# The last projection of a hybrid encoder layer: operand sums moved from DRAM to on-chip memory, weight blocks loaded fewer times, residual added by DMA

## The chip, the cores and the metric

The kernel runs on one core of a Trainium2 chip. The metric is the device time of one execution in microseconds (us); the median of several runs is quoted. A profile is one further execution, taken by the hardware profiler.

## What is computed

The reference is one layer of a bidirectional encoder with 512 tokens and a width of 2048, in float32: an input projection, a Mamba-2 style branch, an attention branch, a gated merge, one output product with a residual, and a last RMSNorm. The part that the change touches is its end:

```python
merged = jax.nn.sigmoid(g_ssm) * (y @ w_proj_ssm) + jax.nn.sigmoid(g_attn) * (o @ w_proj_attn)
return x + merged @ w_out
...
return rmsnorm(x, final_norm_w)
```

`merged` is 512 x 2048 and `w_out` is 2048 x 2048.

## The kernel before

**Engines and splitting.** TensorE (PE) multiplies, VectorE (DVE) and ScalarE (ACT) do elementwise work, GpSimd (POOL) a little of it, and SP issues plain loads. Float32 operands are split into a high and a low part, each of a type that PE takes in one pass, and a product is three matmuls (high x high, high x low, low x high). The high part of a weight chunk is a cast on ACT (`wh`, L434) and the low part a subtraction on DVE (`wl`, L435). So each chunk of 128 x 1024 weights costs one ACT and one DVE instruction before PE can use it.

**Strassen.** Each of the three 2048-wide projections at the end (`wps`, `wpa`, `wo`) is done by the class `Strassen` (L612) with seven block products in place of eight, in Winograd's form. Tokens are halved, the inner dimension is halved, and the output columns are taken in two pairs, `cp` 0 and 1, each of which is halved again. A block product (`product`, L571) is four weight chunks of 512 KB by two banks of 128 tokens: 48 matmuls of 128 x 512. The operands made of the input are x11, x12, x21, x22 and the sums S1 to S4. The weight blocks are W11, W12, W21 and W22, and the sums are T1 = W11 + W12, T2 = T1 + W22, T3 = W22 + W12 and T4 = T2 + W21. (Signs are folded in elsewhere.) P1 takes x11 and W11; P2 x12 and W21; P5 S1 and T1; P6 S2 and T2; P3 S4 and W22; P7 S3 and T3; P4 x22 and T4.

**Weight tiles.** On-chip tiles for weights come in rings: four `X` (T1, T2 and T4 are made in place in them), four `Y` (W22, then T3), and three `wraw`, a ring that raw operands also use. T1 and T3 are made by a second DMA that adds into the tile (`w_more`, L511, issued by POOL, L514). T2 (L716) and T4 (L720) are additions on DVE. For `wps` and `wpa`, T1 and T3 are prepared early in DRAM scratch.

**The order in the output product before.** `wo` first runs a head (L673): P1 and P2 for cp 0, then P1 and P2 for cp 1 (named P1b and P2b), which need only x11 and x12. Then `pair` runs P5, P6, P3, P7, P4 for cp 0 and the same five for cp 1. For this W11 of cp 0 is loaded twice (for P1 and again for T1), W21 twice for each cp, and T1 of cp 1 is written to DRAM scratch (`T_wo`, jobs in `t_jobs`, L486, issued by POOL when P5 of cp 0 is done) and read back.

**The operands before.** `done_pa` (L1439) ends each block of `wpa`: gate, add, and, one product later, eight transposes on PE (`turn`, L1446) whose result gives pieces of x11, x12, x21 or x22 of the merged matrix. Pieces of x11, x12 and x22 are split at once or reloaded; the sums S1 to S4 are put together in DRAM (`m_d`) by DMAs that add (L1455, L1462), with two copies of S3 inside DRAM as starting values of S2 and S4 (L1475), and each sum is then read back into raw tiles and split. The last piece, of x22, is turned when P1 of `wo` is through, so S1, S2 and S4 are complete only after that. The tiles for turned pieces, for gates and for residual blocks are one ring of three (`st`, L382).

**The residual before.** For each of the 16 output blocks of 128 x 512, `fetch_o` (L1588) loads the block of x into an `st` tile, DVE adds it (L1607), ACT squares it for the norm (L1600), and POOL multiplies it by the last gain (L1603). Of the two blocks of the last product (`last_o`, L1633) the addition is done before the product. `finish` (L1618) normalises 128 tokens and stores them.

**What orders the work.** PE runs in program order. On the other engines a scheduler orders by program order and by given priorities (`AHEAD`, `LOAD_AHEAD`), and `keep_in_program_order` holds an instruction at its place. Each engine's queue, SP's and POOL's DMA issues among them, is then carried out strictly in order. `hooks` name work to be put behind a given product, as in

```python
wo = Strassen("wo", m_ops, -1, done_o, fetch_o, {
    (0, "P1"): [s_loads], (0, "P2"): [lambda: wo.first_columns(0, nc.sync, True)],
    (1, "P1"): [MC("S1"), MC("S2"), LP(m_ops, "S4")], (0, "P5"): [MC("S4"), final_weights, t_made],
    (1, "P3"): [lambda: finish(0)], (1, "P7"): [lambda: finish(1)]}, kept_o, last_o)
run(wo.head())
run(wo.pair(0, True))
run(wo.pair(1, True))
```

Of the kernel before, what the change touches and what calls it, by code (L numbers as in the profile page):

```python
# [72 lines left out]
def build(tc, a):  # L73
# [48 lines left out]
    m_d = {w: scratch(f"m_{w}", 2048) for w in ("x11", "S1", "S2", "S3", "S4")}  # L122
# [4 lines left out]
    t_d["wo", 1, "T1"] = scratch("T1_wo1", 4096)  # L127
# [323 lines left out]
    class Ops:  # L451


        def __init__(self, src, blocked=False):
            self.src, self.raws, self.view, self.blocked = src, {}, {}, blocked
# [4 lines left out]
        def split(self, which, op, in_order=False):  # L460
            for q, t in enumerate(self.raws.pop(which)):
                ks = slice(4 * q, 4 * q + 4)
                h, l, raw = op[:, 0, ks], op[:, 1, ks], view4(t)
                i = split_into(h, l, raw, -1 if which == "S2" else 1)
                if in_order:
                    tc.keep_in_program_order(i)
            self.see(which, op)

        def see(self, which, op):
            if self.blocked:  # L470
                op = op.rearrange("p s (q t k) (u c) -> p s q t (k u) c", q=2, t=2, u=2)
                self.view[which] = lambda s, j, i: op[:, s, j // 4, i, j % 4]
            else:
                self.view[which] = lambda s, j, i: op[:, s, j, i * P:(i + 1) * P]
# [137 lines left out]
    class Strassen:  # L612
# [35 lines left out]
        def first_columns(self, cp, queue=nc.sync, both=False):  # L648

            self.ahead[cp] = [self.columns(w_tile("X"), cp, m, queue, both) for m in range(4)]  # L650

        def columns(self, t, cp, m, queue=nc.sync, both=False):

            if self.made(cp, "T1"):
                return t_load(t, self.w, cp, "T1", m, queue)
            w_load(t, self.w, cp, 0, 0, m)
            if both:
                w_more(t, self.w, cp, 0, 1, m, LOAD_AHEAD)
            return t
# [13 lines left out]
        def head(self):  # L673

            a = evict((yield from self.first(0, "P1")), "p1")
            self.hook(0, "P1")
            yield from self.second(0, a, lambda i: self.kept("C11", 0)("p5", i))
            self.hook(0, "P2")
            b = evict((yield from self.first(1, "P1b")), "kk")
            self.hook(1, "P1")  # L680
            self.p1 = (a, b)
            yield from self.second(1, b, lambda i: self.kept("C11", 1)("p5", i), None, "P2b")
            self.hook(1, "P2")

        def pair(self, cp, headed=False):
# [8 lines left out]
            if headed:  # L694
                p1 = self.p1[cp]
            else:
                p1 = evict((yield from product(
                    "P1", self.op("x11"), (lambda m: w_load(w_tile("X"), w, cp, 0, 0, m)) if made else column,
                    None if made else lambda m, raw: w_more(raw, w, cp, 0, 1, m))), "p1")
                self.hook(cp, "P1")  # L700

# [25 lines left out]
            def t3(m, raw):  # L727
                w_more(raw, w, cp, 0, 1, m)
                if headed:
                    t4_alone(m, raw)  # L730
# [4 lines left out]
            u = p1 if headed else [sum_tile("u") for _ in range(2)]  # L735
# [4 lines left out]
            if not headed:  # L740
# [698 lines left out]
    def done_pa(t, b, o):  # L1439
# [3 lines left out]
        def turn():  # L1443
# [3 lines left out]
            o_ = st("turned")  # L1447
            w, q = f"x{t // 2 + 1}{b // 2 + 1}", 2 * (b % 2) + t % 2
            d = {n: m_d[n][:, q * SEQ:(q + 1) * SEQ] for n in m_d}
            if b < 2:  # L1450
                act.copy(o_, tp)
                for n in ("x11", "S3") if t < 2 else ("S1",):
                    put(d[n], o_)
                if t >= 2:
                    pool.dma_start(d["S3"], o_, accum_op=ALU.add)  # L1455
            else:
                h, l = (m_op[w][:, s_, 2 * q:2 * q + 2].rearrange("p k t -> p (k t)") for s_ in range(2))
                act.activation(o_, tp, AF.Copy, scale=-1.0)
                act.activation(h, tp, AF.Copy, scale=-1.0)
                dve.scalar_tensor_tensor(l, tp, -1.0, h.bitcast(F32), ALU.mult, ALU.subtract)  # L1460
                for n in ("S4",) if t < 2 else ("S1", "S2", "S4"):
                    pool.dma_start(d[n], o_, accum_op=ALU.add)  # L1462
# [3 lines left out]
    m_op = {}  # L1466
    m_ops = Ops(m_d, True)

    def m_place(w):
        def f():  # L1470
            m_op[w] = slot(w)
            m_ops.see(w, m_op[w])
        return f

    def m_copies():  # L1475
        for n in ("S2", "S4"):
            tc.keep_in_program_order(pool.dma_start(m_d[n], m_d["S3"]))

    def MC(w):
        return lambda: m_ops.split(w, m_op[w], True)  # L1480
# [3 lines left out]
    def o_sums(n, i=1):  # L1484
# [12 lines left out]
        (1, "P1"): [LP(m_ops, "x11"), m_place("x11")], (1, "P5"): [MC("x11"), m_place("S1")],  # L1497
        (1, "P6"): [m_place("S2"), m_copies], (1, "P2"): [m_place("x12"), LP(m_ops, "S3")],
        (1, "P3"): [m_place("S3")], (1, "P7"): [m_place("x22"), MC("S3"), m_place("S4")]})
# [86 lines left out]
    res, room = {}, {}  # L1586

    def fetch_o(t, b):  # L1588
        fetched[t, b] = st("gate")
        pool.dma_start(fetched[t, b], a["x"][t * P:(t + 1) * P, b * SEQ:(b + 1) * SEQ])  # L1590

    def kept_o(tag, cp, i):
        if tag == "C11":
            return sum_tile(("p5", "ms")[cp])
        if "big" not in room:
            room["big"] = xa.tile([P, 2, 2, 2, SEQ], F32, tag="opa", bufs=2, name="big")
        return room["big"][:, int(tag == "C22"), cp, i]

    def squares(t, b):
        act.activation(fetched.pop((t, b)), res[t, b], AF.Square, accum_out=ssf[:, t, b:b + 1])  # L1600

    def weigh(t, b):
        pool.tensor_mul(res[t, b], res[t, b], room["fw"][:, b])  # L1603

    def done_o(t, b, o):
        res[t, b] = o
        dve.tensor_add(o, o, fetched[t, b])  # L1607
        squares(t, b)
        if "fw" in room:
            weigh(t, b)  # L1610

    def final_weights():
        room["fw"] = xa.tile([P, 4, SEQ], F32, tag="opa", bufs=2, name="fw")
        act.dma_start(room["fw"], a["fnw"].rearrange("o (b n) -> o b n", b=4).broadcast_to([P, 4, SEQ]))
        for t, b in list(res):
            weigh(t, b)

    def finish(t):  # L1618
# [4 lines left out]
        for b in (2, 0, 1, 3):  # L1623
            o = res[t, b]
            if b == 2 and t >= 2:
# [23 lines left out]
    def s_loads():  # L1649
        with tc.high_priority(offset=AHEAD):  # L1650
            for w in ("S1", "S2"):
                m_ops.raws[w] = [col_tile("Y", "xraw") for q in range(2)]
                for q in range(2):
                    pool.dma_start(m_ops.raws[w][q], m_d[w][:, q * 1024:(q + 1) * 1024])

    wo_jobs = t_jobs("wo")

    def t_made():
        while wo_jobs:
            tc.keep_in_program_order(wo_jobs.popleft()())  # L1660

    wo = Strassen("wo", m_ops, -1, done_o, fetch_o, {
        (0, "P1"): [s_loads], (0, "P2"): [lambda: wo.first_columns(0, nc.sync, True)],
        (1, "P1"): [MC("S1"), MC("S2"), LP(m_ops, "S4")], (0, "P5"): [MC("S4"), final_weights, t_made],
        (1, "P3"): [lambda: finish(0)], (1, "P7"): [lambda: finish(1)]}, kept_o, last_o)
    run(wo.head())
    run(wo.pair(0, True))
    run(wo.pair(1, True))
# [69 lines left out]
```

## Time and profile before

| | us |
|---|---|
| median of 3 runs | 2063.26 |
| lowest, highest | 2059.05, 2070.34 |
| the profiled execution, its own time | 2067.23 |
| span of that execution's profile (first to last instruction) | 2065.5 |
| busy: PE, DVE, ACT, POOL | 1952.0, 1539.9, 1004.5, 377.8 |

Every time in a profile counts from the start of its span. A line of a view of waits names who waited, at which line of the kernel, for whom, with the total, the count and the longest wait in us. A line of the chain gives start, duration and what the time went to. "Issue" in the chain is time in which the engine waited for nothing that the profile shows. The granted clock (PEclk) is the share of PE's full clock. The DMA share is the mean busy share of 16 DMA engines.

### The profile page before, as it was taken

Reading aid. Unit: us, or ns where it says so; the run is one execution under the profiler, and the core shown is the slowest. Engines: PE = TensorE matmul, PEld = TensorE weight load, DVE = VectorE, ACT = ScalarE, POOL = GpSimd, SP = SyncE. Lnnn points to the kernel's source line nnn. Section 1 sums busy time; section 2 is a strip of 40 time slices with the busy share of each in tenths; the row PEclk is TensorE's granted clock in tenths of the full one; section 3 lists DMA queues with packets and bytes.
Section 4 is the critical chain, followed back from the end, with each engine's and each line's share of the span. In section 5 each row is a group of like instructions: output and inputs, shape, how many; then the busy total and the mean of one; then the engine's idle time right before and its main releaser. Section 6 shows DMA issues by size and latency. Waiting matters only on the chain.

```text
span 2065.5 us, 24821 instructions
## 1 busy us (share of the span) xinstructions
PE 1952.0 (95%) x8978; PEld 1605.2 (78%) x8978; DVE 1539.9 (75%) x2018; ACT 1004.5 (49%) x1398; POOL 377.8 (18%) x417
## 2 busy tenths in 40 slices
PE   6999999999999999999999999999999999987877
PEld 4878888888878788787788888888777778875666
DVE  7976676676669799898794866767577888774767
ACT  6444444444445646546455444444445445443344
POOL 0001010010032252332520111100120110131222
PEclk9999999999999999999999999999999999998989
DMA  5467657657547757687465966953587886889575
GB/s 195 166 177 200 177 122 190 192 120 177 143 165 196 216 164 210 204 248 227 143 188 173 250 166 178 246 134 93 148 275 221 277 326 232 283 245 278 153 204 138
DMA packets 172074, 404.79 MB, mean 196 GB/s; under 512 B 17104, under 2 KB 62288, under 8 KB 171728
## 3 DMA queue, kind: packets, MB, share of 16 engines
q1 hardware_dynamic: 104976, 239.38, 35.3%
q0 software_dynamic: 36032, 121.13, 26.4%
q10 hardware_dynamic: 30944, 42.71, 5.7%
q8 instruction: 70, 1.15, 0.2%
q14 instruction: 52, 0.43, 0.1%
HBM read 344.95 MB, written 110.62 MB: 221 GB/s over the span
## 4 chain that ended last, share of the span: by engine, by line
PE 64%; DVE 15%; DMA 10%; issue 6%; ACT 4%; POOL 1%; ACTq 0%; SPq 0%; DVEq 0%; POOLq 0%
PE P L588 10%; PE P L589 10%; PE P L587 10%; DVE wl L435 3%; PE za L169 2%; PE za L170 2%; PE za L171 2%; DVE sum L1078 2%; PE xbc L169 2%; PE xbc L170 2%; PE xbc L171 2%; DVE wl L165 1%; DMA m_S<-turned 1%; PE pb L1355 1%; DMA wraw<-wo 1%
## 5 line engine op out<-in xcount | busy, mean ns | idle before, releaser
L434 ACT CAST wh<-X 128x1024 fp32r<-128x1024 f32 x172 | 180.6, 1053 | 201.0 <-PE P L589 151.8
L435 DVE TENSOR_TENSOR wl<-X,wh 128x1024 fp32r<-128x1024 f32 x172 | 212.5, 1239 | 85.8 <-ACT wh L434 85.1
L165 DVE TENSOR_TENSOR wl<-wraw,wh 128x1024 fp32r<-128x1024 f32 (+2 forms) x148 | 177.2, 1198 | 83.5 <-ACT wh L164 81.3
L164 ACT CAST wh<-wraw 128x1024 fp32r<-128x1024 f32 (+2 forms) x150 | 145.0, 969 | 129.9 <-PE xbc L170 35.4
L435 DVE TENSOR_TENSOR wl<-Y,wh 128x1024 fp32r<-128x1024 f32 x96 | 118.3, 1234 | 85.6 <-ACT wh L434 85.6
L434 ACT CAST wh<-Y 128x1024 fp32r<-128x1024 f32 x96 | 101.0, 1053 | 147.5 <-PE P L589 102.7
L169 PE MATMUL xbc<-h_h,wh 128*128 128x512 f32 x384 | 151.6, 395 | 0.0
L171 PE MATMUL xbc<-h_h,wl 128*128 128x512 f32 x384 | 149.9, 390 | 0.0
L170 PE MATMUL xbc<-h_l,wh 128*128 128x512 f32 x384 | 149.7, 390 | 0.0
L587 PE MATMUL P<-wh,h_h 128*128 128x512 f32 x384 | 149.4, 389 | 0.0
L588 PE MATMUL P<-wl,h_h 128*128 128x512 f32 x384 | 149.4, 389 | 0.0
L589 PE MATMUL P<-wh,h_l 128*128 128x512 f32 x384 | 149.4, 389 | 0.0
L435 DVE TENSOR_TENSOR wl<-wraw,wh 128x1024 fp32r<-128x1024 f32 x64 | 78.2, 1223 | 59.4 <-ACT wh L434 59.4
L434 ACT CAST wh<-wraw 128x1024 fp32r<-128x1024 f32 x64 | 67.3, 1052 | 108.2 <-PE P L589 53.0
L588 PE MATMUL P<-wl,S 128*128 128x512 f32 x288 | 112.4, 390 | 0.8 <-DVE wl L435 0.6
L589 PE MATMUL P<-wh,S 128*128 128x512 f32 x288 | 112.1, 389 | 0.0
L587 PE MATMUL P<-wh,S 128*128 128x512 f32 x288 | 112.0, 389 | 0.0
L169 PE MATMUL za<-h_h,wh 128*128 128x512 f32 x256 | 101.5, 396 | 0.0
L170 PE MATMUL za<-h_l,wh 128*128 128x512 f32 x256 | 99.9, 390 | 0.0
L171 PE MATMUL za<-h_h,wl 128*128 128x512 f32 x256 | 99.9, 390 | 0.0
L1078 DVE TENSOR_TENSOR_SCAN sum<-da,scn 128x512 f32<-128x512 f32 x64 | 86.3, 1362 | 0.0
L1342 ACT ACTIVATE pr<-s,nm 128x512 f32<-128x512 f32 x64 | 44.1, 689 | 84.6 <-DVE nm L1340 83.8
(726 smaller groups left out, 5292.0 us busy)
## 6 DMA issues: line engine op xcount, KB each, us to landing
wraw<-wi SPq DMA_DIRECT2D x102, 512.0 KB, 4.0
T_wps<-wps POOLq DMA_DIRECT2D x32, 512.0 KB, 6.2
da<-da_d SPq DMA_DIRECT2D x64, 256.0 KB, 4.5
T_wpa<-wpa POOLq DMA_DIRECT2D x32, 512.0 KB, 9.4
wraw<-wps SPq DMA_DIRECT2D x24, 512.0 KB, 5.9
wraw<-wo SPq DMA_DIRECT2D x24, 512.0 KB, 6.1
xbc_d<-xbc ACTq DMA_DIRECT2D x24, 256.0 KB, 3.1
wraw<-wun SPq DMA_DIRECT2D x16, 384.0 KB, 3.2
```

The lines of the kernel that those rows point to most:

```text
L164: act.copy(h, raw)
L165: (dve if ahead[0] else pool).tensor_sub(l, raw, h.bitcast(F32))
L169: pe.matmul(out, wh, xh, start=start, stop=False)
L170: pe.matmul(out, wh, xl, start=False, stop=False)
L171: pe.matmul(out, wl, xh, start=False, stop=stop)
L434: i = act.copy(hi_, raw)
L435: dve.tensor_sub(lo_, raw, hi_.bitcast(F32))
L587: pe.matmul(bs[i], xh, wh, start=(j == 0), stop=False)
L588: pe.matmul(bs[i], xh, wl, start=False, stop=False)
L589: pe.matmul(bs[i], xl, wh, start=False, stop=(j == 7))
L1078: dve.tensor_tensor_scan(sums[dd], flat(da), mask, 0.0, ALU.add, ALU.mult)
L1342: act.activation(pr, s, AF.Exp, bias=nm, scale=SCALE, accum_out=sm_)
```

## The change

- **Order.** The head is gone. For cp 0 the order is P1, P2, P5, P6, P3, P7, P4, and for cp 1 it is P1, P5, P6, P2, P3, P7, P4. PE does the same 14 products.
- **Weights.** P1 loads W11 straight into the X tiles; W12 is added into them by DMA for T1 while P1 runs. In cp 1, W21 is loaded once, for P2 and T4 together; in cp 0 it is still loaded twice. No T1 goes through DRAM.
- **Operands.** Only x11, x21 and S3 still go to DRAM. Raw tiles of S1 (from x21), S2 and S4 (from S3) and S3 are loaded from there; S4's in one place of the operand ring that also holds the raw of x22. The turned pieces of x12 are added by DMA into S4's raw tile on chip; the pieces of x22 are subtracted from S1's raw tile by DVE straight out of PE's banks, written to x22's raw tile, and added by DMA into the raw tiles of S2 and S4. S2 is split behind P2 of cp 0, S4 and x22 behind P5, S3 behind P6.
- **Residual.** For 12 of the 16 blocks POOL issues a DMA that adds x into the finished block, and ACT squares it one product later. Only the four blocks of the last 256 tokens and columns of cp 1 keep the old way. The last gain is loaded behind P2 of cp 1 instead of P5 of cp 0; for the first 256 tokens it is multiplied in by DVE in `finish`.

The core of the diff:

```diff
-    m_d = {w: scratch(f"m_{w}", 2048) for w in ("x11", "S1", "S2", "S3", "S4")}
+    m_d = {w: scratch(f"m_{w}", 2048) for w in ("x11", "x21", "S3")}
...
-    t_d["wo", 1, "T1"] = scratch("T1_wo1", 4096)
...
+        def load(self, which, src, tiles):
+            self.raws[which] = tiles
+            for q, t in enumerate(tiles):
+                tc.keep_in_program_order(pool.dma_start(t, src[:, q * 1024:(q + 1) * 1024]))
+
+        def raw(self, which, q, t):
+            return self.raws[which][q][:, t * SEQ:(t + 1) * SEQ]
+
+        def into(self, which, raw, c0, n):
+            h, l = (self.tile[which][:, s_, c0:c0 + n] for s_ in range(2))
+            return split_into(h, l, raw, -1 if which == "S2" else 1)
+
+        def split(self, which):
+            for q, t in enumerate(self.raws.pop(which)):
+                tc.keep_in_program_order(self.into(which, t, q * 1024, 1024))
...
-        def pair(self, cp, headed=False):
+        def pair(self, cp, headed=False, early=False):
...
                     None if made else lambda m, raw: w_more(raw, w, cp, 0, 1, m))), "p1", self.kept("p1", cp))
                 self.hook(cp, "P1")
+                if early:
+                    yield from self.second(cp, p1, lambda i: self.kept("C11", cp)("p5", i))
+                    self.hook(cp, "P2")
...
                 w_more(raw, w, cp, 0, 1, m)
-                if headed:
+                if early:
                     t4_alone(m, raw)
...
+            elif t < 2:
+                o_ = st("turned")
+                act.activation(o_, tp, AF.Copy, scale=-1.0)
+                pool.dma_start(m_ops.raw("S4", q, u), o_, accum_op=ALU.add)
+                m_ops.into(w, o_, sl.start, SEQ)
             else:
...
+                s1, raw = (m_ops.raw(n, q, u) for n in ("S1", "x22"))
+                dve.tensor_sub(s1, s1, tp)
+                act.activation(raw, tp, AF.Copy, scale=-1.0)
+                m_ops.into("S1", s1, sl.start, SEQ)
+                for n in ("S2", "S4"):
+                    pool.dma_start(m_ops.raw(n, q, u), raw, accum_op=ALU.add)
...
+        (1, "P1"): [m_place("x11"), m_load("x11", "x11", w_raw)], (1, "P5"): [m_split("x11"), m_room],
+        (1, "P6"): [m_place("S1")], (1, "P2"): [m_place("x12")], (1, "P3"): [m_place("S2")],
+        (1, "P7"): [m_place("S4"), m_load("S1", "x21", y_tile), m_load("S2", "S3", y_tile)],
+        (1, "P4"): [m_place("x22")]})
...
     def done_o(t, b, o):
         res[t, b] = o
-        dve.tensor_add(o, o, fetched[t, b])
-        squares(t, b)
-        if "fw" in room:
+        if late(t, b):
+            dve.tensor_add(o, o, fetched[t, b])
+            squares(t, b)
             weigh(t, b)
+            return
+        pool.dma_start(o, x_of(t, b), accum_op=ALU.add)
+
+        def then():
+            squares(t, b)
+            if "fw" in room:
+                weigh(t, b)
+            if b == 3:
+                finish(t)
+
+        after(1, then)
...
     wo = Strassen("wo", m_ops, -1, done_o, fetch_o, {
...
+        (0, "P2"): [m_split("S2")],
+        (0, "P5"): [m_split("S4", "x22"), m_place("S3"), m_load("S3", "S3", w_raw)],
+        (0, "P6"): [m_split("S3")], (1, "P2"): [final_weights]}, kept_o, last_o)
+    run(wo.pair(0, early=True))
+    run(wo.pair(1))
```

More of the change, by code (lines that the diff above doesn't have):

```diff
@@ new lines, in done_pa, with m_place, m_room, m_load @@
+        after(1, turn)
+    m_ops = Merged()
+    def m_place(*which):
+        return lambda: [m_ops.place(w, slot(w)) for w in which]
+    def m_room():
+        t = xb.tile([P, 4, 1024], F32, tag="opb", bufs=4, name="m_raw")
+        n_places[0] += 1
+        m_ops.raws["x22"] = [t[:, q] for q in range(2)]
+        m_ops.load("S4", m_d["S3"], [t[:, 2 + q] for q in range(2)])
+    def m_load(w, src, tile_):
+        return lambda: m_ops.load(w, m_d[src], [tile_("xraw") for q in range(2)])
+    def y_tile(name):
+        return col_tile("Y", name)
```

131 lines of the change are left out of this document (50 added, 81 removed).

## The prediction

> **What bounds the kernel now.** I read the page first, then the busy time by stretch, the waits of PE, the chain, and the waits of the other engines.
>
> ```profile
> span 2065.5 us, 24821 instructions
> ## 1 busy us (share of the span) xinstructions
> PE 1952.0 (95%) x8978; PEld 1605.2 (78%) x8978; DVE 1539.9 (75%) x2018; ACT 1004.5 (49%) x1398; POOL 377.8 (18%) x417
> ```
>
> PE is busy for 95% of the span, so only stretches where it starves can give time back. I looked for them by cutting the output product at its block products. In order the rows are P1, P2, P1b, P2b, P5 with P6, P3, P7 (all cp 0), and the last row holds six products: P4 of cp 0 and all five of cp 1.
>
> ```profile
> core 0: us, PE busy (x) PEld busy (x) DVE busy (x) ACT busy (x) POOL busy (x), PEclk, DMA share, GB/s
> 1841.20:1861.90 20.70, 14.42 (x58) 11.19 (x57) 8.70 (x11) 7.01 (x9) 8.31 (x11) 0.84 1.05 311
> 1861.90:1873.20 11.30, 11.30 (x52) 9.07 (x51) 6.19 (x6) 6.25 (x10) 5.89 (x7) 1.00 1.09 278
> 1873.20:1897.80 24.60, 13.32 (x49) 9.86 (x47) 6.18 (x8) 5.57 (x9) 4.24 (x8) 0.83 0.90 285
> 1897.80:1923.70 25.90, 18.23 (x48) 12.62 (x49) 13.78 (x12) 9.76 (x11) 0.00 (x0) 0.77 0.55 171
> 1923.70:1945.50 21.80, 21.80 (x97) 18.02 (x96) 18.84 (x17) 12.53 (x16) 8.30 (x6) 1.00 0.34 120
> 1945.50:1959.10 13.60, 11.40 (x49) 8.74 (x47) 11.07 (x11) 3.15 (x3) 6.26 (x9) 1.00 0.94 254
> 1959.10:1986.90 27.80, 14.54 (x49) 10.92 (x50) 10.18 (x11) 6.69 (x9) 7.08 (x8) 0.75 0.99 251
> 1986.90:2052.80 65.90, 65.66 (x289) 53.77 (x287) 57.62 (x73) 34.63 (x50) 19.49 (x19) 1.00 0.51 141
> ```
>
> The last row is the yardstick: six products in 65.90 us with PE busy throughout, 10.98 us each. The whole output product takes 2052.80 - 1841.20 = 211.6 us. Fourteen products at 10.98 are 153.8. Behind P1 come the last eight transposes,
>
> ```profile
> 1861.15 1.04 PE L1446 MATMUL turn<-cst,u 128*128 128x128 f32 x8
> ```
>
> whose end overlaps with the next matmul, so I allow 0.8 for them, which makes 154.6. So **57.0 us are lost**: about 9 in P1 (20.7 less 11.0 and 0.8), 13.6 in P1b, 14.9 in P2b, 2.6 in P3 and 16.8 in P7. The clock column belongs to this: it falls to 0.75 to 0.84 in the rows that starve, so each wait costs more than its own length. Before this stage PE does not starve, and after it 2065.5 - 2052.8 = 12.7 us are a tail of elementwise work and stores:
>
> ```profile
> 1780.00:1841.00 61.00, 60.83 (x280) 50.18 (x279) 52.18 (x60) 29.64 (x34) 12.17 (x19) 1.00 0.76 219
> ```
>
> The waits of PE over the stage say which engine it waited for, and the chain says what that engine waited for:
>
> ```profile
> PE P L587 <- ACT wh L434: 17.1, 3, 12.0
> PE P2b L587 <- ACT wh L434: 9.8, 4, 4.9
> PE P1b L588 <- DVE wl L435: 6.4, 1, 6.4
> ```
>
> ```profile
> 1847.39 17.60 DMA m_S<-turned
> ...
> 1866.59 7.49 DMA m_S<-turned
> 1874.08 7.04 issue
> 1881.12 3.44 DMA xraw<-m_S
> ...
> 1947.30 8.20 DMA T_wo<-wo
> ...
> 1963.27 10.72 DMA Y<-wo
> ```
>
> PE lacks weight splits, and those lack data: first the sums in DRAM and their way back (m_S, xraw), then the scratch copy of T1 (T_wo), behind which the DMA that makes T3 (Y<-wo) stood in POOL's queue. DVE itself stood still for loads that it takes in order, ahead of later splits:
>
> ```profile
> DVE p L1607 <- DMA gate<-x: 13.7, 2, 7.0
> DVE u L1440 <- DMA gate<-ga_d: 7.3, 2, 5.6
> ```
>
> **The change part by part.** Sizes and times to landing of the transfers in this stage:
>
> ```profile
> wraw<-wo SPq DMA_DIRECT2D x20, 512.0 KB, 5.5
> gate<-x POOLq DMA_DIRECT2D x16, 256.0 KB, 4.0
> ```
>
> *Head taken out, S sums on chip.* The causes of the loss in P1b and P2b go: the sums' round trip through DRAM, the loads held behind it on SP, and DVE's 13.7 us at the residual loads, since a DMA now adds x and ACT looks at the result one product (10.98 us) later, against 4.0 us to land. That is 13.6 + 14.9 = 28.5 us, if nothing else is late. What is late next is dealt with under the front, below.
>
> *T1 of cp 1 not through DRAM.* Eight transfers leave POOL's queue ahead of T3's, so the losses of P3 and P7, 2.6 + 16.8 = 19.4 us, lose their cause. T1 of cp 1 is then made like T3: by adding DMAs issued during P1 and used in the very next product. The nearest row is T3 of cp 1, in the yardstick stretch:
>
> ```profile
> L514 POOL DMA_DIRECT2D Y<-wo x4: 853/866/897, 2019.4 to 2027.4; - x4
> ...
> DMA to landing us min/median/max: 5.6/7.1/7.3
> ```
>
> These four landed in 5.6 to 7.3 us and PE lost nothing. So T1 of cp 1 costs 0 if POOL's queue is free, and up to the 16.8 of P7 if it isn't; it could hardly gain, as before this step had its scratch copy in time. I take 0.
>
> *W11 straight into X.* Before, these four loads went first, for a use three products away, and those for P1 came behind them:
>
> ```profile
> 1825.86 9.47 SPq L478 DMA_DIRECT2D X<-wo  x4
> ```
>
> Now the early loads are the ones that P1 uses, which should end most of P1's 9 us. What stays is DVE's wait of 7.3 us for the gates of the last `wpa` block: their `st` tiles still wait for turned pieces to be added elsewhere. I leave 4 of it (bounds 0 and 9).
>
> *The front.* S1 is made by DVE in time (two subtractions and two half-width splits in the 11 us of P2). S2 is the new wait: its two ACT splits are pinned behind P2 and wait for adding DMAs that can be issued only after the turn behind P1, and the casts for P5 stand behind them on ACT; PE waits for these. Behind S2's split stand also the loads of W22 into the two Y tiles that S2's raws hold, on SP. No row shows an adding DMA from on-chip memory into on-chip memory. From one side, adds into weight tiles landed in 7.1 us (above), which P2's 11 us hide. From the other, the DRAM sums issued in the crowd of P1 needed
>
> ```profile
> DMA to landing us min/median/max: 13.0/17.5/19.4
> ```
>
> 17.5 us, which from about 1855 (P1's end at 1853, the turn, the issue) gives 1872, 8 us behind P5's start at 1841.2 + 11.0 + 0.8 + 11.0 = 1864. By bytes: between the first X load at 1826 and 1864 the new order wants 18 transfers of 512 KB (W11, W12 and W21 four each, raws of S1 and S2 four, half of W22 two) and 14 of 256 KB (gates and their addends four, adds ten), 13.1 MB; at the 285 GB/s of P1b's row that is 46 us, to 1872 as well. Most of it is not urgent, so I take the middle, **4 us**, and keep 0 and 13 (8, and 5 for W22 behind it). The Trainium skill (page "DMA: Bandwidth & Descriptors", section "Anatomy of one DMA — SWDGE (gpsimd) path") puts most of a DMA's fixed cost in the receipt from the target memory, with HBM the slowest target; by that the adds into on-chip tiles would land sooner than the DRAM rows and this term would be near 0, for a sum 4 lower; no run shows such a transfer yet.
>
> *DVE.* From the turn behind P1 to the end of P3, four products or 44 us, it has 16 weight splits, eight T sums and eight operand splits of 1024 columns, beside shorter work:
>
> ```profile
> L435 DVE TENSOR_TENSOR wl<-wraw,wh 128x1024 fp32r<-128x1024 f32 x15 | 18.4, 1223 | 25.9 <-ACT wh L434 25.9
> ```
>
> All are operations on 1024 columns like this one: 32 x 1.22 = 39 us of 44. Some can wait (T4, x22), so I add 2.5 (bounds 0 and 5).
>
> *Last gain behind P2 of cp 1.* Four POOL products then stand near T3's adds of cp 1. Before, four took 3.54 + 4.51 = 8.05 us:
>
> ```profile
> 1938.27 3.54 POOL L1603 TENSOR_TENSOR p<-p,fw 128x512 f32<-128x512 f32 x2 [1.39 <-DVE wl L435]
> 1941.76 4.51 POOL L1603 TENSOR_TENSOR ms<-ms,fw 128x512 f32<-128x512 f32 x2
> ```
>
> If all precede the adds, P7 waits up to 8; if none, 0. I take 2.
>
> *Nothing for the rest.* The extra DVE subtractions and POOL loads before 1841 lie beside a PE that never starved there (DVE 52.18 of 61.00 us); were that cover gone, two more half-width DVE operations and four load issues would cost some 3 us. The tail keeps its steps, so 12.7 stays; moving part of the gain to DVE lies under P4's 11 us.
>
> **Sum.** 2065.5 - 57.0 + 4 + 4 + 2.5 + 2 = 2021.0 for the span. The median of the runs, 2063.26, is 2.2 below the span (the profiled execution's own time was 2067.23), so the forecast for a median is 2021.0 - 2.2 = **2019 us**.
>
> **Rivals.** *The front stays bound by DMA.* For it: the DMA share is 1.05 and 1.09 in P1 and P2 already, and the two products that covered S2 are gone. Then P1 keeps its 9, S2 and W22 cost 8 + 5, and the 4.5 above stay: 26.5 lost, 2035.0 for the span, 2033. The Trainium skill (same page, section "Rules for kernel authors") says that spreading transfers over the issuing engines gains no bandwidth, since all run on the same 16 DMA engines and interleave. By that rule the operand loads on POOL slow the X loads on SP, which is this rival; the rows of 278 to 311 GB/s at a full DMA share agree with it. Against it: sixteen weight transfers fewer in all.
>
> *POOL's queue takes the place of the waits.* Residual adds wait there for DVE, and T1 and T3 of both pairs stand behind them in order. P7 shows the price of one late set, 16.8 with its slow clock. At three of the four places it is 50.4, the kernel is 6.6 faster, 2057: the change then hardly does what it says. At all four, with S2's 8, it is 75.2, the span is 2065.5 - 57.0 + 75.2 = 2083.7, the time **2081**, slower. It decides from 57.0 / 16.8 = 3.4 places on. For it: P7 of cp 0. Against: T3 of cp 1 with free queue cost nothing, and POOL was busy 19.49 of 65.90 us there.
>
> **How the numbers follow.** Forecast 0.66; front bound by DMA 0.21; three late sets 0.07; four 0.06. About 0.5% (10 us) can be told from no change, so the first two are faster: 0.87, 0.07, 0.06. The low end is the forecast with all four unknowns at their low ends (2019 - 12.5 = 2006.5) and a little run to run spread, 2005. The high end holds the second case with its DVE and POOL terms at their bounds (2033 + 2.5 + 6 = 2041.5) and some spread, 2045.
>
> **What would show it.** Right: the 14 products take some 167 us, with P2, P3 and P4 of either pair at 11; no m_S or T_wo in the chain; no wait of DVE for gate<-x before the last products; a granted clock of 1.0 in most rows. The front: a wait of ACT for S2's raw behind P2, of about 4 us. Wrong: PE waiting for casts of X or Y that wait for adding DMAs (POOL's queue), a DMA share near 1 up to P6 with PE starving (first rival), DVE without idle time before P3 and PE waiting for it, or a start of the stage later than 1841.

## The result and the profile after

The changed kernel takes 2045.04 us (median of 4 runs, 2044.42 to 2046.08) beside 2063.24 for the kernel before: a ratio of 0.9909, 95% interval 0.9881 to 0.9937. It is faster, by 18 of the 44 us that were forecast, and lies just above the upper end of the forecast's range, 2045. The profiled execution took 2045.46. Its page begins:

```profile
span 2043.7 us, 24735 instructions
## 1 busy us (share of the span) xinstructions
PE 1945.2 (95%) x8978; PEld 1602.9 (78%) x8978; DVE 1532.7 (75%) x2016; ACT 1000.6 (49%) x1392; POOL 363.4 (18%) x405
```

The busy time by stretch, cut at the products as before. In order: P1 with the turn, P2, P5, P6, P3, P7, P4 of cp 0; P1 of cp 1; the six products behind it; the tail. The columns are the stretch, its length, the busy time of the five engines, the granted clock, the DMA share and GB/s.

```profile
1842.90:1856.05 13.15, 12.11 (x60) 9.80 (x58) 9.16 (x13) 6.96 (x11) 5.82 (x7) 1.00 1.04 272
1856.05:1874.90 18.85, 11.80 (x52) 8.85 (x49) 6.33 (x8) 6.16 (x9) 3.85 (x5) 0.95 0.96 220
1874.90:1888.70 13.80, 13.13 (x48) 10.36 (x49) 13.80 (x14) 5.93 (x6) 2.46 (x4) 0.83 0.48 132
1888.70:1899.60 10.90, 10.90 (x49) 9.01 (x48) 6.79 (x7) 9.76 (x14) 0.37 (x1) 1.00 0.45 124
1899.60:1911.90 12.30, 11.17 (x49) 8.93 (x48) 10.08 (x11) 6.30 (x7) 3.47 (x4) 1.00 0.88 182
1911.90:1931.75 19.85, 13.91 (x50) 10.88 (x49) 12.60 (x13) 4.20 (x4) 1.74 (x2) 0.83 0.87 260
1931.75:1948.00 16.25, 13.04 (x49) 10.13 (x48) 7.20 (x9) 6.55 (x12) 2.58 (x3) 0.89 0.78 205
1948.00:1959.40 11.40, 11.07 (x49) 8.82 (x47) 3.44 (x4) 4.50 (x8) 4.37 (x5) 1.00 0.99 171
1959.40:2028.40 69.00, 66.26 (x288) 53.90 (x288) 54.14 (x69) 30.54 (x41) 15.56 (x17) 1.00 0.48 117
2028.40:2043.70 15.30, 0.14 (x1) 0.00 (x0) 6.82 (x22) 5.10 (x12) 1.26 (x1) 0.66 0.46 154
```

Against 10.98 a product (and 0.8 for the turn) the stage loses 30.9 us: P1 1.4, P2 7.9, P5 2.8, P3 1.3, P7 8.9, P4 5.3, P6 and cp 1 together 3.4. The forecast had 12.5. The tail is 15.3 in place of 12.7, and the stage starts at 1842.9 in place of 1841.2: 2021.0 - 12.5 + 30.9 + 2.6 + 1.7 = 2043.7, the span. The start says nothing of the change; in the runs below it lies between 1837 and 1847, so that kernels are compared from the stage's start.

What PE, ACT and DVE waited for in the stage (total, times, longest):

```profile
PE P L606 <- DVE wl L434: 11.8, 8, 5.9
PE P L605 <- ACT wh L433: 10.3, 5, 4.8
...
ACT wh L433 <- DMA Y<-wo: 9.9, 5, 4.5
ACT scr L1639 <- DMA big<-x: 9.8, 3, 6.5
...
ACT scr L1639 <- DMA p<-x: 7.5, 4, 3.7
ACT scr L1639 <- DMA kk<-x: 7.1, 2, 5.2
ACT S__15292 L436 <- DMA xraw<-m_raw: 7.0, 1, 7.0
...
DVE X L734 <- DMA wraw<-wo: 5.5, 1, 5.5
```

No T_wo is left in the chain, and PE still lacks weight splits. But now fewer of the splits are late for their own data (ACT's casts wait 9.9 us for pieces of T3, `Y<-wo`, and 5.4 us for one of W21); for the rest ACT and DVE stand, in their order, at something else. ACT stands 7.0 us at S2's split (L436) and 24.4 us at squares (L1639) of blocks into which x is still being added; DVE stands 5.5 us at the sum for T4 (L734). The chain shows two of them, the adds of S2 and the reload of W21, and the last fetch of x:

```profile
1859.24 13.51 DMA xraw<-m_raw
...
1905.64 9.57 DMA wraw<-wo
...
2027.62 3.26 DMA gate<-x
```

### The profile page after: what moved, and what is told of

It is laid out like the page before. It is cut to its first block, busy times and chain, and to the rows that moved or that the text cites. A ratio compares the mean times of both kernels' runs of the same rounds, so it can differ in the third digit from the quotient of the medians.

```text
span 2043.7 us, 24735 instructions
## 1 busy us (share of the span) xinstructions
PE 1945.2 (95%) x8978; PEld 1602.9 (78%) x8978; DVE 1532.7 (75%) x2016; ACT 1000.6 (49%) x1392; POOL 363.4 (18%) x405
## 4 chain that ended last, share of the span: by engine, by line
PE 65%; DVE 13%; DMA 9%; issue 7%; ACT 3%; POOL 1%; SPq 0%; ACTq 0%; DVEq 0%; POOLq 0%
PE P L606 11%; PE P L607 11%; PE P L605 11%; PE za L168 2%; PE xbc L168 2%; PE za L169 2%; PE xbc L169 2%; PE za L170 2%; PE xbc L170 2%; DVE sum L1092 2%; DVE wl L434 2%; DVE wl L164 1%; DMA stack<-qr 1%; DMA wraw<-wps 1%; PE pb L1369 1%
## 5 line engine op out<-in xcount | busy, mean ns | idle before, releaser
L434 DVE TENSOR_TENSOR wl<-X,wh 128x1024 fp32r<-128x1024 f32 x180 | 219.4, 1223 | 100.9 <-ACT wh L433 100.8
L433 ACT CAST wh<-X 128x1024 fp32r<-128x1024 f32 x180 | 188.9, 1053 | 203.2 <-PE P L607 162.1
L434 DVE TENSOR_TENSOR wl<-Y,wh 128x1024 fp32r<-128x1024 f32 x96 | 117.1, 1223 | 79.1 <-ACT wh L433 79.1
L433 ACT CAST wh<-wraw 128x1024 fp32r<-128x1024 f32 x56 | 58.9, 1052 | 81.9 <-PE P L607 55.9
L434 DVE TENSOR_TENSOR wl<-wraw,wh 128x1024 fp32r<-128x1024 f32 x56 | 68.4, 1223 | 39.6 <-ACT wh L433 39.6
```

What stands on the lines that cost most here:

```text
L433: i = act.copy(hi_, raw)
L434: dve.tensor_sub(lo_, raw, hi_.bitcast(F32))
```

## The experiments

The theory from this trace: three terms of the sum failed, S2's adds, the reload of W21 for T4, and the squares that stand on ACT behind the residual's adds; a fourth, in the tail, comes with the first two finishes, whose eight DVE operations now stand ahead of the last residual adds. Its rival: DMA or DVE bounds the stage, and each repair only moves the loss. The table is from the busy time by stretch and the starts of the products, in us; each kernel's median is beside its ratio to the kernel before on the same chip.

| kernel | P1 | P2 | P5 | P6 | P3 | P7 | P4 | cp 1 | tail | stage | median | ratio |
|---|---|---|---|---|---|---|---|---|---|---|---|---|
| changed | 13.2 | 18.9 | 13.8 | 10.9 | 12.3 | 19.9 | 16.3 | 80.4 | 15.3 | 200.8 | 2045.0 | 0.9909 |
| e4, four edits | 11.8 | 12.3 | 12.2 | 12.2 | 11.6 | 13.4 | 20.7 | 85.9 | 14.2 | 194.3 | 2038.1 | 0.9854 |
| e13, squares later | 13.0 | 18.7 | 13.7 | 10.9 | 10.9 | 18.0 | 10.9 | 79.1 | 16.0 | 191.1 | 2035.8 | 0.9862 |
| e12, order only | 13.1 | 13.6 | 10.9 | 15.8 | 10.9 | 18.5 | 10.9 | 79.6 | 15.6 | 188.9 | 2030.9 | 0.9839 |
| e11, residual old | 16.5 | 11.4 | 10.9 | 12.1 | 13.4 | 17.6 | 10.9 | 79.0 | 11.7 | 183.4 | 2024.4 | 0.9809 |
| e9, pinned squares | 11.8 | 12.2 | 12.3 | 10.9 | 10.9 | 12.3 | 10.9 | 80.4 | 16.3 | 177.8 | 2019.2 | 0.9786 |
| e15, best | 11.8 | 12.3 | 12.2 | 10.9 | 10.9 | 12.2 | 10.9 | 79.2 | 12.4 | 172.8 | 2014.6 | 0.9751 |

**One repair at a time.** *e1: the reload of W21 from P3 to P7.*

```
             def t3(m, raw):
                 w_more(raw, w, cp, 0, 1, m)
-                if early:
-                    t4_alone(m, raw)
...
-            A = yield from product("P7", self.op("S3"), c7, t4_alone if headed and made3 else None, self.pre(2, 2 * cp + 1))
+            A = yield from product("P7", self.op("S3"), c7, t4_alone if headed and made3 or early else None, self.pre(2, 2 * cp + 1))
```

> The reload of W21 for T4 of cp 0 is moved from P3 to P7, where S3's raws have left the wraw ring. Theory A (DVE stood 5.55 us at this reload, in order ahead of a split that P7 needed): P7 of cp 0 falls from 19.85 us to 11.5, the time from 2045.0 to 2037. Rival B (the adds of W12 that make T3 land late, in a DMA crowd, and P7 would wait for them anyway): P7 stays above 17 us, the time within 2 us of 2045.

Measured: 2042.57, ratio 0.9884 (0.9849 to 0.9919). P7 falls from 19.85 to 13.5, most of the way to the 11.5 expected, but P4 rises from 16.25 to 19.7, where ACT stands 9.5 us at the squares of `kk`, and cp 1 takes 3.9 us more; the time misses theory A's 2037. The reload did hold P7; what it gave is lost behind it.

*e2: cp 0's squares called two products after their adds, not one.*

```
-        after(1, then)
+        after(1 if b >= 2 else 2, then)
```

> The squares of the eight residual blocks of cp 0 come two products behind their adding DMA instead of one. Theory A (ACT stood 5.16 and 1.93 us at squares whose DMA had not landed, with the casts for P4 behind them): P4 of cp 0 falls from 16.25 us to 11.2, the time from 2045.0 to 2040. Rival B (P4 waits because its X chunks are made late, T4 being late): P4 stays above 15 us, the time at 2045.

Measured: 2042.89, ratio 0.9881 (0.9840 to 0.9922). P4 falls to 12.9, but P1, P5 and P7 of cp 1 take 13.7, 14.7 and 16.0. The call is later; the place in ACT's queue isn't, as e4 and e9 show.

*e3: S2's last four pieces subtracted by DVE from PSUM, not added by DMA.*

```
                 dve.tensor_sub(s1, s1, tp)
+                s2 = m_ops.raw("S2", q, u)
+                dve.tensor_sub(s2, s2, tp)
...
-                for n in ("S2", "S4"):
-                    pool.dma_start(m_ops.raw(n, q, u), raw, accum_op=ALU.add)
+                pool.dma_start(m_ops.raw("S4", q, u), raw, accum_op=ALU.add)
```

> The four pieces of x22 are subtracted from S2's raw tile by DVE, straight out of PE's banks, as S1's are, instead of being added by DMA; S4's stay with DMA. Theory A (the adds into S2's raw landed 13.5 us after their issue, ACT stood 6.95 us at its split with the casts for P5 behind it): P2 falls from 18.85 us to 13.7 (2.7 of waiting for W21 stay), P5 from 13.8 to 11.0, the time from 2045.0 to 2037. Rival B (the front is bound by the bytes to be moved, S2 only shows it first): W22 and W21 come late in its place, P2 and P5 together fall by less than 3 us, the time above 2042.

Measured: 2035.94, ratio 0.9847 (0.9812 to 0.9881). P2 and P5 in its busy time by stretch:

```profile
1849.20:1861.50 12.30, 11.55 (x51) 8.99 (x49) 8.71 (x11) 7.18 (x10) 1.72 (x2) 1.00 0.99 225
1861.50:1873.70 12.20, 11.77 (x50) 8.70 (x48) 9.95 (x11) 4.47 (x6) 2.84 (x4) 1.00 0.85 238
```

24.5 us in place of 32.65, at a clock of 1.00 in place of 0.95 and 0.83: the front's loss came with S2's adds.

*e4: the three, and `finish(0)` and `finish(1)` called behind P7 of cp 1.*

> The three edits of the runs before it together, and a fourth: the normalisation of the first 256 tokens is put behind the additions of the last blocks on DVE, as a hook of P7 of cp 1. If the four losses are separate, as theory A has it: 8 for T4, 5 for the squares, 8 for S2 and 2.6 for the tail (15.3 us from the last matmul to the end, 12.7 in the kernel before), 23.6 less than 2045.0, 2021. Rival B (one crowd of DMA behind all of them, so that what is taken from one place comes back at the next): 2035 or more.

Measured: 2038.05, ratio 0.9854 (0.9818 to 0.9890), not better than e3 alone; its expectation of an additive gain missed. P7 is at 13.4, P4 at 20.7. Over the stage ACT waits:

```profile
ACT scr L1638 <- DMA p<-x: 12.2, 4, 5.4
ACT scr L1638 <- DMA kk<-x: 10.4, 2, 7.7
ACT scr L1638 <- DMA big<-x: 10.4, 3, 7.6
ACT scr L1638 <- DMA ms<-x: 8.9, 2, 4.9
```

41.9 us of ACT's time at squares, with casts behind them. Earlier casts don't help, as ACT only reaches the squares sooner. The call of the squares of `kk` stands behind P4, yet on ACT they stand between P4's first and second cast of X:

```profile
1908.78 1.04 ACT L433 CAST wh<-X 128x1024 fp32r<-128x1024 f32 x1 [0.49 <-PE P L607]
1917.57 0.63 ACT L1638 ACTIVATE scr<-kk 128x512 f32<-128x512 f32 x1 [7.74 <-DMA kk<-x]
...
1921.58 2.92 ACT L433 CAST wh<-X 128x1024 fp32r<-128x1024 f32 x3
```

That is a new theory: the squares are what is late next wherever another wait goes.

**Where it goes next.** *e6: e4, with the residual the old way* (`late(t, b)` always true: x fetched, added by DVE, squared at once).

> The changed kernel with S2 by DVE, the reload of W21 one product later and the first two finishes behind P7 of cp 1, and with the residual the old way: x is fetched into a tile, DVE adds it, ACT squares at once. Theory A (what kept the three edits from adding up is ACT, which stands in order at squares of blocks whose adding DMA has not landed): ACT's waits for p, kk, ms and big from x go, P4 of cp 0 falls from 20.7 us to at most 14, the stage from its start to the end of the span falls from 194.2 to 182 to 188, the time to 2024 to 2032. Theory B (the loss is carried by the loads of the weights or by DVE and appears wherever the slack is least, whichever engine takes the wait): the stage stays at 190 or above, the time above 2032, with DVE standing at the fetched x instead.

*e7: e4, with the squares of the 12 blocks left out.*

> The same three edits, the residual by adding DMAs as in the changed kernel, but the squares of the 12 blocks that get x by DMA are left out (their sums of squares are set to 1, so the norm's factors differ): no instruction of ACT waits for those DMAs in the stage. Theory A (ACT's in-order squares are the price): P4 of cp 0 at 11 to 13 us, the stage from its start to the end of the span at 180 to 185, some 2022 to 2027 us. Theory B (the adding DMAs delay the weights, or DVE does): the stage at 190 or above, over 2032, with P4 still above 15.

Measured, on the same chip: 2025.61 (0.9813, 0.9786 to 0.9839) and 2019.92 (0.9788, 0.9758 to 0.9818); the stage takes 183.2 and 174.8 us, P4 10.9 in both. Theory A holds. In e7 the adding DMAs are all there; without ACT's wait for them P4's loss is gone and the stage is 19.5 us shorter than e4's, 4.4 of it in the tail.

*e8: no adds of W12 behind P1 of cp 0.*

> The changed kernel without the four adding DMAs of W12 into X behind P1 of cp 0 (T1 of cp 0 is left as W11, so what P5 multiplies by differs): 2 MB less in the crowd in which S2's adds land, nothing else changed. Theory (the crowd sets the 11 to 14 us to landing of S2's adds): they land within 9 us, P2 and P5 of cp 0 take 25 to 28 us together in place of 32.65. Rival (an add between on-chip tiles issued behind the turn is slow by itself or waits in POOL's queue): landing and both products stay within 1.5 us of the changed kernel's.

Measured: 2036.60 (0.9866, 0.9839 to 0.9893); P2 and P5 take 11.8 and 12.9. S2's and S4's adds behind the turn, first in the changed kernel, then here (KB each, median us to landing):

```profile
m_raw<-m_raw POOLq DMA_DIRECT2D x4, 256.0 KB, 13.5
xraw<-m_raw POOLq DMA_DIRECT2D x3, 256.0 KB, 13.5
```

```profile
xraw<-m_raw POOLq DMA_DIRECT2D x2, 256.0 KB, 5.1
m_raw<-m_raw POOLq DMA_DIRECT2D x2, 256.0 KB, 6.8
```

The same transfers land in 5 to 7 us without the 2 MB of W12 beside them: the crowd sets 13.5. The W12 adds stand in POOL's queue as S2's do, so this run doesn't separate waiting behind them there from sharing the DMA engines with them. That the crowd reaches another queue shows in SP's three loads of W22 and W21 beside them: 7.1 to 9.2 us in the changed kernel, 4.7 to 6.9 here.

*e5: on the kernel before, T1 of cp 1 made by adding DMAs in X; nothing else.*

> The kernel before with one part of the change alone: T1 of cp 1 is made by adding DMAs into the X tiles in place of eight transfers through a DRAM scratch. The order, the head and the residual stay as before. Theory (the prediction's term): P3 and P7 of cp 0 lose 19.4 us before only because the scratch copies stand in POOL's queue ahead of T3; they then take 11 to 13 us each, and T1 of cp 1 costs nothing: some 2046 us, 0.991 of before. Rival: another set of adds in POOL's queue behind P1 of cp 1 makes its users late at the price of one late set, 16.8: then 2060, no change.

Measured: 2056.77, ratio 0.9967 (0.9948 to 0.9986), between the two expectations. P3, P7, P4 of cp 0, then P5 and P6 of cp 1 (whose P1 runs in the head, in this order):

```profile
1942.40:1955.05 12.65, 11.23 (x49) 8.93 (x48) 12.65 (x13) 4.21 (x4) 5.72 (x6) 1.00 0.83 171
...
1965.95:1976.90 10.95, 10.95 (x49) 8.81 (x47) 5.79 (x8) 2.84 (x4) 3.89 (x5) 1.00 1.00 362
1976.90:1995.05 18.15, 13.62 (x50) 10.62 (x50) 13.93 (x13) 7.45 (x10) 6.39 (x6) 0.81 0.68 144
1995.05:2006.95 11.90, 11.15 (x49) 8.92 (x48) 10.87 (x9) 9.59 (x12) 2.57 (x3) 1.00 0.21 73
```

P3 and P7 fall from 41.4 us to 23.6 (P7, the stretch from 1955.05, takes 10.9): 17.8 of the forecast's 19.4. T1's own adds are late in this order (ACT's casts of X wait 15.0 us for them from 1966 on) and cost 18.15 + 11.90 - 21.96 = 8.1, so 9.7 stay, near the 8.5 of the medians. In the changed kernel P1 of cp 1 takes 11.4 and P5 12.0 (its start to P6's): there the term is 1.4 at most.

**The order of ACT.** *e9: e4, with cp 0's squares three products later, pinned there (cp 1's four are pinned too, one product later as before).*

```
-            squares(t, b)
+            tc.keep_in_program_order(squares(t, b))
...
-        after(1, then)
+        after(1 if b >= 2 else 3, then)
```

> S2 by DVE, the reload of W21 one product later, the first two finishes behind P7 of cp 1, the residual by adding DMAs, and the squares of cp 0's eight blocks three products after their adds, pinned in that place on ACT behind the casts that come before them in the program; all work is done. Theory A (the price of the residual by DMA is only where ACT's squares stand in its order): P4 of cp 0 at 11 to 14 us in place of 20.7, the stage from its start to the end of the span at 180 to 188, 2022 to 2030 us. Rival (the adding DMAs themselves hold up the weights' loads): P4 above 15 or another product takes the loss, the stage at 190 or above, over 2032.

Measured: 2019.18, ratio 0.9786 (0.9761 to 0.9811). P3, P7 and P4 of cp 0:

```profile
1886.92:1897.80 10.88, 10.88 (x50) 9.01 (x48) 9.27 (x11) 5.78 (x9) 2.69 (x4) 1.00 0.97 197
1897.80:1910.06 12.26, 11.49 (x50) 8.85 (x48) 9.63 (x10) 4.21 (x4) 1.74 (x2) 1.00 0.99 314
1910.06:1920.94 10.88, 10.88 (x50) 9.01 (x48) 5.77 (x7) 3.16 (x3) 1.72 (x2) 1.00 1.05 322
```

All work is done, every adding DMA stays, and P4 takes 10.88 at a DMA share of 1.05: here a full DMA did not starve PE, with ACT's queue letting the casts pass. The edit pins the squares and moves them one product on from e4; no run separates the two. Of ACT's waits at squares only cp 1's three are left:

```profile
ACT scr L1639 <- DMA big<-x: 10.8, 3, 6.8
```

*e11: the changed kernel with the residual alone put back (and the finishes later).*

> The changed kernel with the residual alone put back the old way (x fetched, added by DVE, squared at once; the first two finishes behind P7 of cp 1), everything else as changed. Theory A: P4's loss of 5.3, the tail's 2.6 and some 2 us in cp 1 go, DVE stands little for the fetched x since no sums go through DRAM any more: 2033 to 2039 us. Rival (in the crowd of cp 0 DVE stands at the fetched x as it did before, 13.7 us): no gain, 2043 or above.

Measured: 2024.38, ratio 0.9809 (0.9783 to 0.9835), much better than either expectation, since P2 and P5 fell to 11.4 and 10.9 too, though S2's last add lands later there (1875.7, in the changed kernel 1872.8). ACT around P5 (start, length, operation, idle time before it), first the changed kernel, then e11:

```profile
1872.84 1.06 ACT L436 ACTIVATE S__15292<-xraw 128x1024 fp32r<-128x1024 f32 x1 [6.95 <-DMA xraw<-m_raw]
1873.80 1.03 ACT L433 CAST wh<-X 128x1024 fp32r<-128x1024 f32 x1
```

```profile
1865.44 2.19 ACT L433 CAST wh<-X 128x1024 fp32r<-128x1024 f32 x2
1869.68 1.06 ACT L433 CAST wh<-X 128x1024 fp32r<-128x1024 f32 x1 [2.05 <-PE P L607]
1872.40 1.05 ACT L433 CAST wh<-X 128x1024 fp32r<-128x1024 f32 x1 [1.66 <-PE P L607]
...
1875.78 1.99 ACT L436 ACTIVATE S__15292<-xraw 128x1024 fp32r<-128x1024 f32 x2
```

In the changed kernel S2's split stands ahead of the first cast of X for P5; in e11 four casts stand ahead of it. By this, not the landing but what is queued behind the wait made the loss. The next two runs test that with every DMA as it is.

*e13: the changed kernel with e9's squares and e4's finishes only.*

> The changed kernel with only the squares of cp 0's blocks three products later, pinned, and the first two finishes behind P7 of cp 1; S2's splits stand where they stood. Theory A: P4 of cp 0, cp 1 and the tail give back 5 + 2 + 2.5 us, P2, P5 and P7 of cp 0 keep theirs: 2033 to 2038 us. Rival (S2's splits in P5 were late only because of the squares too): 2030 or below.

*e12: e13, and S2's splits pinned behind the fourth of P5's casts.*

```
                     dve.tensor_add(raw, raw, Y[m])
+                if m == 3:
+                    self.hook(cp, "P5mid")
...
-        (0, "P2"): [m_split("S2")],
+        (0, "P5mid"): [m_split("S2")],
```

> The changed kernel with every DMA and every operation on its own engine left as it is: only two groups of ACT's (and DVE's) instructions stand later in their queues. S2's splits stand behind four of P5's weight casts instead of ahead of them, and the squares of cp 0's blocks three products after their adds, pinned there; the first two finishes stand behind P7 of cp 1. Theory A (the loss is the order on ACT): P2 and P5 of cp 0 at 22 to 26 us together in place of 32.65, P4 at 11 to 14 in place of 16.25, 2020 to 2029 us. Rival (the transfers, late in the crowd whatever stands before them, keep the loss; the reload of W21 too): the two products stay above 29 or the loss moves into P6 and P7, 2034 or above.

Measured: 2035.80 (0.9862, 0.9844 to 0.9880) and 2030.85 (0.9839, 0.9822 to 0.9856). P2, P5 and P6 of e12:

```profile
1853.84:1867.48 13.64, 11.62 (x52) 9.02 (x50) 8.04 (x10) 6.00 (x8) 3.85 (x5) 1.00 1.09 262
1867.48:1878.36 10.88, 10.88 (x50) 9.01 (x48) 10.04 (x10) 6.60 (x7) 2.83 (x4) 1.00 0.82 168
1878.36:1894.16 15.80, 13.09 (x50) 10.08 (x48) 11.76 (x11) 9.70 (x11) 0.00 (x0) 0.89 0.39 149
```

The order alone is worth 14.2 us by the medians: 9.2 for the squares (with the finishes) and 5.0 for S2's splits, at the same times to landing (S2's last took 13.5, to 1870.5). By the stage it is 9.7 and 2.2, as the start lies 2.3 us earlier in e12's profile, and the intervals of e13 and e12 overlap: S2's order is worth 2 to 5 us. e12 came out just above its own expectation, and the rival has its share: P2 and P5 fall by 7.9 from e13, but P6 takes 15.8 in place of 10.9, because S2's raws stay in two Y tiles until they are split, the loads of W22 wait for these, and DVE then waits 4.2 us for them. That is the "5 for W22 behind it" of the prediction's upper bound. P7 keeps the reload of W21. Taking S2's adds and the reload away (e12 to e9) gives another 11.7.

**What is left.** *e10: e6, with the products with the last gain made by DVE, not POOL* (`dve.tensor_mul` in `weigh`).

> The kernel with the three edits and the residual the old way, and the products with the last gain (eight of 128x512, behind P2 of cp 1) made by DVE in place of POOL. In the run with POOL's products, two weight splits of 1024 columns took DVE 7.97 us in place of 2.4 while POOL made four of them, and P7 of cp 1 took 15.2 us. Theory (an elementwise operation of POOL holds DVE up): P7 of cp 1 falls to 11 to 12.5, the time to 2020 to 2023. Rival (the W12 adds for T3, which land 8.2 to 8.7 us after their issue, make ACT's casts late): P7 of cp 1 stays above 14, the time at 2025.

Measured: 2018.97 (0.9779, 0.9752 to 0.9806). P7 of cp 1 falls from 15.15 us to 10.90, and the stage from 183.2 to 179.0, as the theory had it; the ratio's interval overlaps that of e6. *e14: e9 with the same edit.*

> The kernel with S2 by DVE, the reload of W21 one product later, the finishes later and the pinned squares, with the products with the last gain made by DVE in place of POOL. Each gain was seen alone: if they add, P7 of cp 1 falls from 13.7 us (P3's end to P4's start) to 11 to 12, and the time from 2019.2 to 2015 to 2018. If POOL's products were hidden there, it stays at 2019.

Measured: 2019.16 (0.9779, 0.9760 to 0.9798), no gain over e9. In P7 of cp 1 ACT's squares of cp 1's blocks stand there as well (11.9 us, 7.0 in one piece), and hide it. *e15: e14 with cp 1's four blocks fetched and added by DVE* (`late(t, b)` is `b >= 2`).

> As the run with S2 by DVE, the reload of W21 later, pinned squares, later finishes and DVE's products with the last gain, but the residual of cp 1's four first blocks fetched and added by DVE as in the last four; cp 0's eight keep the adding DMAs. Theory A (ACT's squares standing at adding DMAs cost cp 1 too: 6.8 to 7.0 us of wait in one piece behind P3): P7 of cp 1 falls from 14.0 us (P3's end to P4's start) to 11 to 12, the tail behind the last matmul from 15.6 to 11 to 13, the time from 2019 to 2011 to 2015. Rival (the finishes behind P7 and the gates' tiles make the tail): no change, 2017 to 2020.

Measured: 2014.55, ratio 0.9751 (0.9730 to 0.9772), as theory A had it, though the interval overlaps e14's; by the stage it is 172.8 against 177.7. P7, P4 of cp 1 and the tail:

```profile
1977.20:1989.30 12.10, 11.26 (x50) 8.94 (x49) 10.30 (x27) 5.97 (x10) 1.10 (x2) 1.00 0.57 149
1989.30:2000.30 11.00, 11.00 (x49) 8.81 (x47) 11.00 (x19) 1.45 (x4) 0.54 (x1) 1.00 0.61 207
2000.30:2012.70 12.40, 0.03 (x1) 0.00 (x0) 5.24 (x20) 4.30 (x10) 0.00 (x0) 0.60 0.50 177
```

This is the fastest version by the medians: the stage loses 172.8 - 154.6 - 12.4 = 5.8 us. One thing stays open: e6 has two edits more than e11 and is no faster, though these edits are worth 11.7 beside adding DMAs. With the fetched x, P2, P5 and P6 of e6 take 13.7, 13.1 and 14.4, each 2 us more than in e11, and P1 4 less; which queue causes it was not tried. These products also vary from one execution to the next: e10, which has e6's code up to cp 1, shows 12.2, 14.6 and 11.7, and its six runs lie between 2013.0 and 2025.0.

## Why the prediction was wrong

**Right.** The losses that the DRAM sums and the scratch copy of T1 caused are gone, and none of that chain came back. e5 put the T1 term at 17.8 of 19.4, and T1's own adds cost at most 1.4 in the new order (0 taken). P1 loses 1.4 (4 taken; its cause is not split further). DVE's 2.5 was not needed: P3's 1.3 goes with the squares (e13). POOL's queue did not take the place of the waits as the second rival had it: POOL waits for DVE's splits, and what stands behind it, ACT's casts of T3, waits 9.9 us in all and 4.5 at most, far from 16.8 a set. The first rival had half the truth: the DMA share is 1.04 in P1, but P1 didn't keep its 9 us.

**S2, taken at 4, measured at 8.2** (e3, of the 10.7 that P2 and P5 lose). The failing step is "most of it is not urgent, so I take the middle". Both bounds were worked out to 1872, from the crowd's landings and from the bytes at 285 GB/s, and the last add of S2 landed at 1872.8. The step that discounted them had no row of its own. The Trainium skill's page "DMA: Bandwidth & Descriptors" (section "Anatomy of one DMA — SWDGE (gpsimd) path"), from which the prediction worked out a term near 0 for an on-chip target, does not decide here: the target was on-chip in both cases, and landing took 5 to 7 us or 13.5 by what else was in flight (e8). The Trainium skill's rule in the same page's section "Rules for kernel authors", that DMAs of different issuing engines interleave on the same 16 DMA engines, agrees with SP's loads in e8 (4.7 to 6.9 us in place of 7.1 to 9.2). What the step also missed is that part of the price, 2 to 5 us net, belongs to the place in ACT's queue (e12), a thing that can be chosen.

**The reload of W21, not priced, measured at 6.3 to 7.6** (e1 and e9, of the 8.9 that P7 loses). The reload isn't new: before, it stood in P3 of cp 0 too, and its four loads, issued from 1919.5 to 1945.2, landed in 3.1 to 3.9 us. New is what stands beside it. S3 was split in `wpa` before, by 1839; now its raws hold two of the three `wraw` tiles until DVE has split them (the first at 1909.7), so two of the four loads are issued at 1905.6 and 1909.8, in the crowd of T3's adds, and land 9.57 and 9.21 us later. The sum for T4 stands ahead of P7's first split on DVE. The prediction counted the loads before 1864 and none behind. e1 and e9 show it: P7 13.5 and 12.3.

**The residual, taken at 0, measured at 9.2 with its order** (e12's and e13's part; 5.3 in P4, the rest in P3, P7 and cp 1), **and at some 20 with all that follows from it** (e11, by the medians; 17.3 by the stage; the finishes stand later there too). The failing step is "ACT looks at the result one product (10.98 us) later, against 4.0 us to land". Both numbers fail. The time runs from DVE's last subtraction, not from the product's end, and DVE made `kk` when the casts of P4 were due; the landing that was taken, 4.0, is the median of 16 plain loads over the whole stage before, of which those issued from 1872.5 to 1885.6, in the crowd, took 11.2 to 12.1; at `kk` the adds took 8.6 and 10.7. And one product later in the program is not one product later on ACT: unpinned squares stood between casts (e2 and e4 called them later and kept waits at them; e9 pinned them, one product later still, and lost those of cp 0). So the change took DVE's 13.7 us at the fetched x away and gave ACT 24.4 us at the squares.

**The last gain, taken at 2, and the tail, taken as unchanged.** The six products on POOL cost 4.3 where nothing hides them (e6 against e10) and nothing beside ACT's waits at squares (e9 against e14); the reason was not POOL's queue, as the prediction had it, but DVE (below). The tail is 2.6 longer. In its chain the finishes' eight DVE operations stand ahead of the last residual adds, these release the `st` tile for the last fetch of x, issued 0.8 us before the last matmul ends, and it lands at 2030.9. But calling the finishes behind P7 did not shorten it: e4, e9, e12 and e13 have 14.2 to 16.3, and in e4 five of the eight operations then stand between the last residual adds and the last subtractions. e15, with no adding DMA in cp 1, has 12.4, and e1 and e2, which leave the finishes where they are, have 12.9 and 12.4. So the cause of the longer tail stays open.

## What to carry to other kernels

A new wait on an in-order engine is priced by what stands behind it in that engine's queue, as the scheduler will really place it, and by a landing time from the crowd at its issue, never by the idle landing and never by the line order of the source. When a repair of one wait gives nothing, look at which instruction of the same engine stands next at a late transfer: here the repairs gave 7 us together (e4) and 26 once the squares were pinned, a product later, behind the casts (e9). And where a bound has been worked out twice from rows and the two agree, take it, not the middle.

## What the runs showed of the hardware

An adding DMA between on-chip tiles of 256 KB took 13.5 us to land in the crowd behind P1, and 5.1 to 6.8 at the same place with 2 MB of other adds gone from the same queue (e8): same target. All are medians.

In e6 POOL's elementwise operations held one of DVE's. DVE's and POOL's operations before P7 of cp 1:

```profile
1983.04 7.97 DVE L434 TENSOR_TENSOR wl<-Y,wh 128x1024 fp32r<-128x1024 f32 x2 [0.43 <-ACT wh L433]
```

```profile
1983.48 2.84 POOL L1635 TENSOR_TENSOR ms<-ms,fw 128x512 f32<-128x512 f32 x2
1985.98 2.80 POOL L1635 TENSOR_TENSOR p<-p,fw 128x512 f32<-128x512 f32 x2
```

The two weight splits, 1.22 us each elsewhere, take 7.97 together; by the records the first takes 6.83 of it and ends 1.1 us behind POOL's fourth product. So, if the records hold, one DVE operation waited through four of POOL's. In the kernel before, three splits beside POOL's products took 2.3 us each in place of 1.22 (1940.6 to 1947.4), while two additions that read one operand from PE's banks kept their 0.68 beside one (1989.5 and 1990.1). The Trainium skill (page "SBUF — State Buffer", section "Terms") says that DVE and GpSimd share a pair of ports that one instruction holds to its end while the other is blocked; the trace agrees, and e6 shows a run of four POOL operations holding DVE for the whole run. e10, with these products on DVE at 0.69 us each, has no such wait.
